# Attention stage of a two-block layer: softmax reciprocals through DRAM, one product per pair of heads

## The chip, the cores and the metric

One core of one Trainium2 chip runs the whole program. The metric is device time in microseconds (us). Names of engines: PE is TensorE's matmul side and PEld its weight loads, DVE is VectorE, ACT is ScalarE, POOL is GpSimd, SP is SyncE, which here issues nearly all DMAs.

## What is computed

The reference is a gated-linear-attention block followed by a second block with two attentions, a convolutional feed-forward layer and norms, on 1024 tokens of width 1024. The change lies in the two attentions of the second block, where each of 8 + 8 heads does, per block of 128 queries,

```python
sc = jnp.where(causal, sc, -jnp.inf)        # or the mask of the 256 selected keys
p = jax.nn.softmax(sc, axis=-1)
o = jnp.einsum('bhqs,bshd->bqhd', p.astype(v.dtype), v)
```

The kernel leaves the division by the softmax sum until after the product with v: with e = exp(sc - max) and l = sum(e), it computes o = (e v) / l.

## The kernel before

The attention stage is `attend` (L1590). It walks over 64 items. An item is a pair of heads (4 pairs of attention "attB", then 4 of "attA"), a head h of the pair and a pair tp of query tiles (t = 2 tp + w, w = 0 or 1), taken in the order tp = 3, 0, 2, 1. Four steps follow each other in a pipeline:

- `stage_a` (two items ahead): the scores of 128 queries in a PSUM tile `pb` of two banks, a DVE pass that adds the mask and takes the row's extreme (L1637 without a loaded mask, L1639 with one, which for attA comes from DRAM by the DMA of L1804 into a ring `mb` of 4), and on ACT the exponential with its row sum (L1640). The row sums go to a column tile `l`.
- `stage_c`, per chunk of 256 keys: up to four 128x128 transposes on PE (L217, the helper `tr`) into a PSUM tile `ps` of a ring of two, and the split of the result into a high and a low part `pt` (ring of 8). In one chunk of three ACT and DVE do this alone (L1658, L1659), in the other two ACT or DVE copies it to a tile of the ring `r2` (L1662) and POOL makes both parts (L1663, L1664).
- `stage_d`, three chunks later: products with v (L1680), collected in `pg` or `po`.
- `finish` (L1686), once per head and half of the queries, 32 times in all: it adds the two halves of `po` (L1693 on ACT, L1695 on DVE), takes the reciprocal of four columns of `l` (L1697), and multiplies. As `l` has queries on partitions and the output `oT` has them along its row, the reciprocals are first spread: four matmuls against the identity with the reciprocal column broadcast as weights (L1700) into a tile of the ring `ps`, a copy to a tile `R` of the ring `r2` (L1702, ACT), and the product on POOL (L1703).

Rings are pools of buffers: an instruction that writes a buffer waits until the last reader of its former content is done. A scheduler fixes each engine's order at build time; on the chip every engine runs its list in order, and so does SP with its DMAs. Behind the stage comes `branches` (L1850), whose first work is the split of the attention outputs (L1865 on ACT, L1867 on DVE and POOL) and which loads gates by DMA (L1875).

Of the kernel before, what the change touches and what calls it, by code (L numbers as in the profile page):

```python
# [6 lines left out]
F32 = mybir.dt.float32  # L7
# [5 lines left out]
OP = mybir.AluOpType  # L13
PSUM = bass.MemoryType.PSUM

P = 128
T = 1024
D = 1024
NT = T // P
# [135 lines left out]
class K:  # L155
# [1434 lines left out]
    def attend(self, jobs, begun, fill):  # L1590

        nc = self.nc

        order = (3, 0, 2, 1)
        items = [(pair, tp, h) for pair in range(4 * len(jobs)) for h in range(2) for tp in order]
        states, live = {}, {}  # L1600
        states[0], todo = begun

        def setup():
            if todo:
                self.ph = "attT"
                todo.pop(0)()
        while todo:
            setup()

        def job(pair):  # L1610
            self.ph = jobs[pair // 4][0]
            return jobs[pair // 4]

        def stage_a(i, w):

            pair, tp, h = items[i]
            if (tp, h, w) == (order[0], 0, 1) and pair + 1 < 4 * len(jobs):
                states[pair + 1], steps = job(pair + 1)[1]((pair + 1) % 4)
                todo.extend(steps)
            t = 2 * tp + w  # L1620
            _, _, score, bias, _, _ = job(pair)
            live["b", pair, t] = bias(t)
            n = self.nk(t)
            off, chunks = self.key_chunks(n)
            z = self.ps2()[:, off:]
            score(states[pair], h, t, z, chunks)
            b = live["b", pair, t]
            if b is None:
                nc.tensor.matmul(z[:, n - P:n], self.idb, self.cb[:, t], start=False, stop=True, skip_group_check=True)
            place, bank = {0: 0, 3: 1, 1: 0, 2: 1}[tp], tp in order[2:]  # L1630
            p, mn = self.g4(), self.col(1, "mn")
            if (place, w) == (1, 1):
                live["l", pair, h, bank] = self.col(4, "l")
            l = live["l", pair, h, bank]
            j = place * 2 + w
            if b is None:
                nc.vector.tensor_scalar(p[:, :n], z[:, :n], 1.0, None, op0=OP.mult, op1=OP.min, accum_out=mn)  # L1637
            else:
                nc.vector.tensor_tensor_reduce(p[:, :n], z[:, :n], b[:, :n], 1.0, 3.0e38, OP.add, OP.min, mn)  # L1639
            nc.scalar.activation(p[:, :n], p[:, :n], AF.Exp, scale=-1.0, bias=mn, accum_out=l[:, j:j + 1])  # L1640
            live["p", i, w] = p

        def tiles(i, c):

            _, tp, _ = items[i]
            return [(s, [w for w in range(2) if s * P < self.nk(2 * tp + w)]) for s in (2 * c, 2 * c + 1)]

        def stage_c(i, c):
            job(items[i][0])
            pt, n = self.ps(), 0  # L1650
            for s, ws in tiles(i, c):
                for w in ws:
                    self.tr(pt[:, n:n + P], live["p", i, w][:, s * P:(s + 1) * P])
                    n += P
            hi, lo = [self.tq.tile([P, 512], F32R, tag="pt", name=self.nm("pt"), bufs=self.bufs["pt"])[:, :n] for _ in range(2)]
            way = (i + c) % 3
            if way == 0:
                nc.scalar.copy(hi, pt[:, :n])  # L1658
                nc.vector.tensor_tensor(lo, pt[:, :n], hi, op=OP.subtract)  # L1659
            else:  # L1660
                x = self.r2()[:, :n]
                (nc.scalar.copy if way == 1 else nc.vector.tensor_copy)(x, pt[:, :n])  # L1662
                nc.gpsimd.tensor_scalar(hi, x, 1.0, 0.0, op0=OP.mult, op1=OP.add)  # L1663
                nc.gpsimd.tensor_tensor(lo, x, hi, op=OP.subtract)  # L1664
            live["pt", i, c] = hi, lo

        def stage_d(i, c):
            pair, tp, h = items[i]
            _, _, _, _, v, _ = job(pair)
            place, bank = {0: 0, 3: 1, 1: 0, 2: 1}[tp], tp in order[2:]  # L1670
            if place == 1 and c == 0:
                live["po"] = self.po() if bank else self.pg()
            po, n = live["po"], 0
            end = self.nk(2 * tp + 1) // P - 1
            x = live.pop(("pt", i, c))
            for s, ws in tiles(i, c):
                o = slice(place * 256 + ws[0] * P, place * 256 + 256)
                w = P * len(ws)
                for j in range(2):
                    nc.tensor.matmul(po[:, o], v(states[pair], h, s), x[j][:, n:n + w], start=(s == 0 and j == 0),  # L1680
                                     stop=(s == end and j == 1), skip_group_check=True)
                n += w
            if s == end and place == 0:
                finish(pair, h, bank)

        def finish(pair, h, bank):  # L1686

            oT, po = job(pair)[5], live.pop("po")
            q = slice(1, 3) if bank else slice(0, 4, 3)
            hs, other = slice(64 * h, 64 * h + 64), slice(64 - 64 * h, 128 - 64 * h)  # L1690
            o = oT[hs, pair % 4].rearrange("p (q t) -> p q t", q=4)[:, q]
            t1, R = self.r2(), self.r2()
            nc.scalar.copy(t1[hs], po[other])  # L1693
            q2 = lambda y: y[hs].rearrange("p (q t) -> p q t", q=2)
            nc.vector.tensor_tensor(o, q2(po), q2(t1), op=OP.add)  # L1695
            rl = self.col(4, "rl")
            nc.vector.reciprocal(rl, live.pop(("l", pair, h, bank)))  # L1697
            pr = self.ps()
            for j in range(4):
                nc.tensor.matmul(pr[hs, j * P:(j + 1) * P], rl[:, j:j + 1].to_broadcast([P, 64]), self.ident,  # L1700
                                 start=True, stop=True)
            nc.scalar.copy(R[hs], pr[hs])  # L1702
            nc.gpsimd.tensor_tensor(o, o, q2(R), op=OP.mult)  # L1703


        for i in range(2):
            for w in (1, 0):
                stage_a(i, w)
            if fill:
                fill.pop(0)()  # L1710
        behind = []
        for i, (pair, tp, h) in enumerate(items):
            nch = self.nk(2 * tp + 1) // 256
            for c in range(nch):
                if i + 2 < len(items):
                    if c == 0:
                        stage_a(i + 2, 1)
                    if c == nch // 2:
                        stage_a(i + 2, 0)
                stage_c(i, c)  # L1720
                behind.append((i, c))
                if len(behind) > 3:
                    stage_d(*behind.pop(0))
            if i % 8:
                setup()
        for x in behind:
            stage_d(*x)
# [291 lines left out]
    def block2_front(self, first):  # L2019

        pool, causal = self.tc.tile_pool, self.causal
        with pool(name=self.nm("kp2"), bufs=1, reuse_waits="tile") as self.kp2:
# [22 lines left out]
                    self.nc.sync.dma_start(self.dbg["mask"], self.maskd)  # L2045
            if self.stop == "topk":
                return
            self.bufs = {"g4": 7, "mb": 4, "pt": 8, "r2": 4}
            with pool(name=self.nm("tq3"), bufs=1, reuse_waits="tile") as self.tq:
                self.attend([job_b, self.block2_a()], (state, steps[6:]),  # L2050
                            self.gate_halves("gA7", lambda: self.g4()[:, :512]))
# [61 lines left out]
```

## Time and profile before

| | us |
|---|---|
| time, median of 3 runs (lowest, highest) | 2461.34 (2451.25, 2475.97) |
| the profiled execution's own time | 2450.84 |
| its span | 2449.0 |
| PE busy over the span | 2310.1 (94%) |
| DVE, ACT, POOL busy | 1421.7, 856.2, 1087.2 |
| the attention stage, first products with v to the last | 1218 to 1523 |

A busy share is a mean over stages with different limits, so the stage of the change is read by itself. An idle time with a releaser says which instruction the engine waited for; only such waits on the engine that sets the pace cost time. PE's weight loads and matmuls overlap, so the time that a group of matmuls holds PE is read from the chain of work, not from the sum of single durations.

### The profile page before, as it was taken

To read this page: it belongs to the slowest core of one execution; us is meant where nothing else is said; L and a number is where in the kernel's file an instruction comes from. 1 tells how busy PE (TensorE), PEld (TensorE's weight loads), DVE (VectorE), ACT (ScalarE), POOL (GpSimd) and SP (SyncE) were. 2 spreads that over 40 slices of the span, in tenths; PEclk is the share of its full clock that TensorE was granted. 3 is DMA by queue.
4 is the path that set the end of the run, shared out by engine and by line. 5 is a ranking of instruction groups with operands and counts; after the bars stand their busy time and mean duration, and the time that the engine had idled before them with its cause. 6 is when DMAs were issued, how large, how long until landed. Compare 5 with 4: busy or idle time off the path is not lost.

```text
span 2449.0 us, 31277 instructions
## 1 busy us (share of the span) xinstructions
PE 2310.1 (94%) x12073; PEld 1909.1 (78%) x12073; DVE 1421.7 (58%) x2151; ACT 856.2 (35%) x1353; POOL 1087.2 (44%) x869
## 2 busy tenths in 40 slices
PE   4999999998898999788999998999999999999997
PEld 3788787786577888666788887788888888888886
DVE  8564457768656467999766666535333333333335
ACT  4454442443313345542366776102211111111111
POOL 5211136554465352335467788530334344443341
PEclk9999999999699999899999999999999999999999
DMA  6222122222332122344420421340111111111112
GB/s 255 90 97 103 73 91 87 82 82 102 129 115 93 68 80 103 143 112 127 155 57 22 119 65 59 110 164 18 69 52 43 49 47 52 52 52 43 52 43 79
DMA packets 119873, 210.44 MB, mean 86 GB/s; under 512 B 45842, under 2 KB 70050, under 8 KB 119330
## 3 DMA queue, kind: packets, MB, share of 16 engines
q1 hardware_dynamic: 119714, 208.34, 24.8%
q8 instruction: 97, 1.59, 0.3%
q14 instruction: 62, 0.51, 0.1%
HBM read 158.46 MB, written 49.84 MB: 85 GB/s over the span
## 4 chain that ended last, share of the span: by engine, by line
PE 54%; DVE 10%; ACT 1%; POOL 1%; issue 1%; DMA 0%; DVEq 0%; POOLq 0%; ACTq 0%; SPq 0%
PE up_pb L1940 5%; PE up_pb L1939 5%; PE up_pb L1938 5%; DVE topk_jk L1550 4%; PE br_ps L1884 3%; PE dn_ps L1993 3%; PE dn_ps L1995 3%; PE dn_ps L1994 3%; DVE topk_r L1547 2%; PE dn_pb L1938 1%; PE dn_pb L1940 1%; PE dn_pb L1939 1%; PE c_ps L242 1%; PE attB_ps L217 1%; PE c_ps L244 1%; PE c_ps L243 1%
## 5 line engine op out<-in xcount | busy, mean ns | idle before, releaser
L1997 DVE TENSOR_TENSOR br_h<-br_h,dn_ps 128x512 f32<-128x512 f32 x176 | 119.6, 685 | 237.5 <-PE dn_ps L1995 237.3
L1976 DVE SCALAR_TENSOR_TENSOR ffn_ws<-up_pb,cols,ffn_ws 128x1023 f32<-128x1023 f32 x66 | 84.5, 1281 | 138.8 <-ACT ffn_ws L1974 138.0
L205 POOL TENSOR_SCALAR up_wh<-up_raw 128x1024 fp32r<-128x1024 f32 x41 | 43.5, 1060 | 272.9 <-PE up_pb L1939 133.9
L210 POOL TENSOR_TENSOR sb_wl<-sb_raw,sb_wh 128x1024 fp32r<-128x1024 f32 x15 | 38.0, 2535 | 189.7 <-ACT sb_wh L209 189.5
L1974 ACT ACTIVATE ffn_ws<-up_pb,cols 128x1024 f32<-128x1024 f32 x33 | 39.9, 1210 | 235.2 <-PE up_pb L1940 235.2
L210 POOL TENSOR_TENSOR up_wl<-up_raw,up_wh 128x1024 fp32r<-128x1024 f32 x41 | 98.5, 2403 | 20.2 <-PE up_pb L1940 17.5
L1938 PE MATMUL up_pb<-br_h,up_wh 128*128 128x512 f32 x264 | 102.7, 389 | 0.0
L1939 PE MATMUL up_pb<-br_h,up_wh 128*128 128x512 f32 x264 | 102.7, 389 | 0.0
L1940 PE MATMUL up_pb<-br_h,up_wl 128*128 128x512 f32 x264 | 102.7, 389 | 0.0
L1938 PE MATMUL up_pb<-op_fh,up_wh 128*128 128x512 f32 x264 | 102.7, 389 | 0.0
L1939 PE MATMUL up_pb<-op_fl,up_wh 128*128 128x512 f32 x264 | 102.7, 389 | 0.0
L1940 PE MATMUL up_pb<-op_fh,up_wl 128*128 128x512 f32 x264 | 102.7, 389 | 0.0
L1548 ACT ACTIVATE topk_r<-topk_r 128x640 bf16<-128x640 bf16 (+1 forms) x64 | 57.4, 898 | 119.6 <-DVE topk_r L1547 119.6
L1981 ACT CAST up_g<-ffn_ws 128x1024 fp32r<-128x1024 f32 x22 | 23.1, 1051 | 176.1 <-PE dn_ps L1994 97.7
L1993 PE MATMUL dn_ps<-dn_wh,up_g 128*128 128x512 f32 x192 | 75.2, 392 | 1.2 <-DVE br_h L1997 1.2
L654 PE MATMUL gla_pb<-QB,gla_X 128*128 128x128 f32 x448 | 68.0, 309 | 8.2 <-DVE QB L641 7.4
L1995 PE MATMUL dn_ps<-dn_wh,up_g 128*128 128x512 f32 x192 | 74.8, 389 | 0.0
L1994 PE MATMUL dn_ps<-dn_wl,up_g 128*128 128x512 f32 x192 | 74.7, 389 | 0.0
L242 PE MATMUL v_ps<-sb_wh,init_hh 128*128 128x256 f32 x256 | 74.3, 291 | 0.0
L244 PE MATMUL v_ps<-sb_wh,init_hl 128*128 128x256 f32 x256 | 74.0, 289 | 0.0
L243 PE MATMUL v_ps<-sb_wl,init_hh 128*128 128x256 f32 x256 | 73.8, 288 | 0.0
L654 PEld LDWEIGHTS gla_pb<-QB,gla_X 128*128 128x128 f32 x448 | 62.6, 218 | 12.5 <-POOL F_ml L762 4.0
(753 smaller groups left out, 7633.5 us busy)
## 6 DMA issues: line engine op xcount, KB each, us to landing
up_raw<-in_wu SPq DMA_DIRECT2D x43, 512.0 KB, 3.4
dn_raw<-in_wu SPq DMA_DIRECT2D x21, 512.0 KB, 3.5
sb_sp<-F_st SPq DMA_DIRECT2D x32, 256.0 KB, 2.0
sb_raw<-in_wu SPq DMA_DIRECT2D x15, 512.0 KB, 4.2
init_X<-in_wada SPq DMA_DIRECT2D x13, 512.0 KB, 5.3
c_raw<-in_wu SPq DMA_DIRECT2D x13, 512.0 KB, 3.5
br_raw<-in_wu SPq DMA_DIRECT2D x12, 512.0 KB, 4.5
bq_raw<-in_wu SPq DMA_DIRECT2D x11, 512.0 KB, 3.8
```

The source lines that it names most:

```text
L210: (nc.gpsimd if pool else nc.vector).tensor_tensor(l, raw, h, op=OP.subtract)
L242: nc.tensor.matmul(po, hh[:, k, ts], wh[:, cs], start=(k == 0), stop=False)
L243: nc.tensor.matmul(po, hh[:, k, ts], wl[:, cs], start=False, stop=False)
L244: nc.tensor.matmul(po, hl[:, k, ts], wh[:, cs], start=False, stop=(k == KT - 1))
L654: self.nc.tensor.matmul(pl[:, cs], X[:, cs], QB[:, cs], start=True, stop=True)
L1938: nc.tensor.matmul(o, wh[:, s], self.hh[h][:, kk], start=(kk == 0), stop=False)
L1939: nc.tensor.matmul(o, wh[:, s], self.hl[h][:, kk], start=False, stop=False)
L1940: nc.tensor.matmul(o, wl[:, s], self.hh[h][:, kk], start=False, stop=(kk == KT - 1))
L1993: nc.tensor.matmul(po, hi[:, ts], wh[:, cs], start=(k == 0), stop=False)
L1994: nc.tensor.matmul(po, hi[:, ts], wl[:, cs], start=False, stop=False)
L1995: nc.tensor.matmul(po, lo[:, ts], wh[:, cs], start=False, stop=(k == 1))
L1997: nc.vector.tensor_tensor(x, x, po, op=OP.add)
```

## The change

`stage_a` now collects the row sums of a whole pair in one tile of 16 columns. With the pair's last exponential, a new function `spread` takes the reciprocal of all 16 columns at once, writes them to DRAM ordered by head and query (4 bytes each, in runs of 32 bytes), and reads them back twice, each head's 1024 values broadcast to 64 partitions, into one tile R of 128x1024. `finish` keeps only the sum of the two halves; with the pair's last half one product of 128x1024 follows, on POOL, for the last pair of all on DVE. R is read with a step of 8 values, since DRAM holds a query's 8 tiles side by side. The rings `mb` and `r2` shrink from 4 to 3 tiles, which makes the room for R.

```diff
-            place, bank = {0: 0, 3: 1, 1: 0, 2: 1}[tp], tp in order[2:]
             p, mn = self.g4(), self.col(1, "mn")
-            if (place, w) == (1, 1):
-                live["l", pair, h, bank] = self.col(4, "l")
-            l = live["l", pair, h, bank]
-            j = place * 2 + w
+            if (tp, h, w) == (order[0], 0, 1):
+                live["l", pair] = self.col(16, "l")
+            l = live["l", pair]
+            j = h * NT + t
...
             live["p", i, w] = p
+            if (tp, h, w) == (order[-1], 1, 0):
+                spread(pair)
+
+        def spread(pair):
+
+            rl = self.col(16, "rl")
+            nc.vector.reciprocal(rl, live.pop(("l", pair)))
+            d = self.dram([2, P, NT], "rld")
+            nc.sync.dma_start(d.rearrange("h q t -> q h t"), rl.rearrange("p (h t) -> p h t", h=2))
+            R = live["R", pair] = self.tq.tile([P, T], F32, tag="R", name=self.nm("R"), bufs=1)
+            for h in range(2):
+                nc.sync.dma_start(R[64 * h:64 * h + 64], bass.AP(tensor=d.tensor, offset=d[h].offset, ap=[[0, 64], [1, T]]))
...
-            t1, R = self.r2(), self.r2()
+            t1 = self.r2()
...
-            rl = self.col(4, "rl")
-            nc.vector.reciprocal(rl, live.pop(("l", pair, h, bank)))
-            pr = self.ps()
-            for j in range(4):
-                nc.tensor.matmul(pr[hs, j * P:(j + 1) * P], rl[:, j:j + 1].to_broadcast([P, 64]), self.ident,
-                                 start=True, stop=True)
-            nc.scalar.copy(R[hs], pr[hs])
-            nc.gpsimd.tensor_tensor(o, o, q2(R), op=OP.mult)
+            if (h, bank) == (1, True):
+                o = oT[:, pair % 4].rearrange("p (t q) -> p t q", t=NT)
+                eng = nc.vector if pair == 4 * len(jobs) - 1 else nc.gpsimd
+                eng.tensor_tensor(o, o, live.pop(("R", pair)).rearrange("p (q t) -> p t q", t=NT), op=OP.mult)
...
-            self.bufs = {"g4": 7, "mb": 4, "pt": 8, "r2": 4}
+            self.bufs = {"g4": 7, "mb": 3, "pt": 8, "r2": 3}
```

On PE, inside the products with v of the first pair of attB (`po` their accumulator, `ps` the transposes' tiles, `pt` the split parts), the kernel before has the four spreading matmuls as row L1700:

```order
L1680 MATMUL attB_po_9518<-attB_pt_9436,attT_vhl_9209 128x256
L1680 MATMUL attB_po_9518<-attB_pt_9462,attT_vhl_9209 128x256
L1700 MATMUL attB_ps_9490<-idr,attB_c_9488 64x128 x4
L1680 MATMUL attB_po_9518<-attB_pt_9463,attT_vhl_9209 128x256
L1680 MATMUL attB_po_9518<-attB_pt_9462,attT_vhl_9209 128x256
```

In the changed kernel the same place (its L1691 is L1680 of before) goes on with the next chunk's transposes:

```order
L1691 MATMUL attB_po_9506<-attB_pt_9434,attT_vhl_9209 128x256
L1691 MATMUL attB_po_9506<-attB_pt_9460,attT_vhl_9209 128x256
L217 MATMUL attB_ps_9497<-idr,attB_g_9395 128x128
L217 MATMUL attB_ps_9497<-idr,attB_g_9386 128x128
L217 MATMUL attB_ps_9497<-idr,attB_g_9395 128x128
L217 MATMUL attB_ps_9497<-idr,attB_g_9386 128x128
L1691 MATMUL attB_po_9506<-attB_pt_9461,attT_vhl_9209 128x256
```

The row of four matmuls is gone, 32 times over the stage, and nothing is added on PE.

On SP, in attA, the changed kernel's queue has the write of the reciprocals (L1649, `rld`) and the two broadcast reads (L1652, `R`) among the loads of masks (L1811, `mb`), where the kernel before has only masks (its L1804):

```order
L1811 DMA attA_mb_12426<-F_maskd_8335 128x640
L1649 DMA attA_rld_12244<-attA_c_12242 128x2x8
L1811 DMA attA_mb_12469<-F_maskd_8335 128x512
L1652 DMA attA_R_12246<-attA_rld_12244 64x1024 x2
L1811 DMA attA_mb_12478<-F_maskd_8335 128x384
L1811 DMA attA_mb_12512<-F_maskd_8335 128x1024
```

Three DMAs per pair are new there, and the reads stand behind a mask load and ahead of others.

On POOL, in the second pair of attB of the changed kernel, the product (L1710) follows the split of v (L1742, L1743) and stands between the two instructions of one chunk (L1674, L1675, which are L1663 and L1664 of before):

```order
L1742 TENSOR_SCALAR attT_vhl_9209<-attT_g_10343 128x16x64
L1743 TENSOR_TENSOR attT_vhl_9209<-attT_g_10343,attT_vhl_9209 128x16x64
L1674 TENSOR_SCALAR attB_pt_10364<-attB_r_10366 128x512
L1710 TENSOR_TENSOR topk_oB_9083<-topk_oB_9083,attB_R_10188 128x1024
L1675 TENSOR_TENSOR attB_pt_10365<-attB_r_10366,attB_pt_10364 128x512
```

Before, the list has four products of 64x512 per pair (L1703) at four places; now it has one of 128x1024. The rows of all engines behind the attention stage are the same in both kernels up to their line numbers, but for the last pair's product, which stands on DVE ahead of the split of the outputs.

## Rows read from the trace of the kernel before

**Rows 1.** The page: span, and each engine's busy time, share and instructions.

```profile
span 2449.0 us, 31277 instructions
PE 2310.1 (94%) x12073; PEld 1909.1 (78%) x12073; DVE 1421.7 (58%) x2151; ACT 856.2 (35%) x1353; POOL 1087.2 (44%) x869
```

**Rows 2.** Windows: length; busy PE, PEld, DVE, ACT, POOL; clock; DMA share, GB/s.

```profile
1218.00:1388.00 170.00, 166.18 (x1225) 147.65 (x1226) 111.85 (x235) 116.91 (x238) 128.02 (x135) 0.98 0.20 56
1388.00:1523.00 135.00, 128.70 (x938) 112.98 (x935) 88.54 (x202) 93.86 (x202) 109.04 (x118) 1.00 0.22 64
1218.00:1523.00 305.00, 294.88 (x2160) 260.63 (x2160) 200.38 (x436) 210.77 (x440) 237.06 (x253) 0.99 0.21 60
```

**Rows 3.** PE's waits, 1218 to 1523: waiter <- releaser: us, times, longest.

```profile
PE attB_pg L1680 <- ACT attB_pt L1658: 1.9, 1, 1.9
PE attB_ps L217 <- ACT attB_r L1702: 1.8, 2, 0.9
...
PE attA_ps L1700 <- ACT attA_r L1662: 1.1, 4, 0.3
...
PE attA_ps L217 <- ACT attA_r L1702: 0.2, 1, 0.2
```

**Rows 4.** The chain of work, 1206 to 1526: start, us, what; first and last full spread.

```profile
1231.16 1.02 PE attB_ps L1700 x8
...
1510.09 1.02 PE attA_ps L1700 x8
```

**Rows 5.** Groups of instructions, 1218 to 1523: count | busy us, mean ns | idle before.

```profile
L1703 POOL TENSOR_TENSOR topk_oB<-topk_oB,attB_r 64x512 f32<-64x512 f32 x16 | 20.5, 1281 | 10.2 <-ACT attB_r L1702 6.8 <-DVE topk_oB L1695 3.0
L1703 POOL TENSOR_TENSOR attT_oA<-attT_oA,attA_r 64x512 f32<-64x512 f32 x15 | 19.3, 1286 | 6.2 <-ACT attA_r L1702 2.8 <-DVE attT_oA L1695 2.6 <-DVE attA_c L1697 0.2
L1702 ACT COPY attB_r<-attB_ps 64x512 f32<-64x512 f32 x16 | 9.3, 580 | 2.7 <-PE attB_ps L1700 1.7 <-POOL attB_pt L1664 0.3
L1736 POOL TENSOR_TENSOR attT_vhl<-attT_g,attT_vhl 128x1024 fp32r<-128x1024 f32 x3 | 7.1, 2375 | 0.2
```

**Rows 6.** POOL's slowest 128x1024 product of the span, and DVE's reciprocals by line.

```profile
L563 POOL TENSOR_TENSOR gs_tmp<-go_qkb,go_qkb 128x1024 f32<-128x1024 f32 x2 | 7.0, 3495 | 3.6 <-DVE go_qkb L798 3.6
L1697 DVE RECIPROCAL attB_c<-attB_c x16: 158/172/179, 1216.8 to 1373.0; 128x4 f32<-128x4 f32 x16
```

**Rows 7.** Waits of ACT's copies: longest for POOL, longest for PE; columns as in 3.

```profile
ACT attA_r L1662 <- POOL attA_pt L1664: 3.2, 2, 2.4
ACT attB_r L1662 <- PE attB_ps L217: 14.5, 12, 3.3
```

**Rows 8.** Timeline of DMA issues and, at the stage's end, of DVE and ACT.

```profile
1539.01 0.27 SPq L299 DMA_DIRECT2D ffn_fd<-fm  x1
1540.14 0.21 SPq L301 DMA_DIRECT2D fr<-ffn_fd  x1
1512.91 0.18 DVE L1697 RECIPROCAL attA_c<-attA_c 128x4 f32<-128x4 f32 x1 [0.78 <-ACT attA_g L1640]
1523.75 0.69 DVE L1695 TENSOR_TENSOR attT_oA<-attA_po,attA_r 64x512 f32<-64x512 f32 x1 [3.21 <-ACT attA_r L1693]
1525.06 6.48 DVE L1867 TENSOR_TENSOR br_ol<-topk_oB,br_oh 128x512 fp32r<-128x512 f32 x4 [0.61 <-ACT br_oh L1865]
1523.75 0.58 ACT L1702 COPY attA_r<-attA_ps 64x512 f32<-64x512 f32 x1
```

**Rows 9.** DMA issue to landing: the masks (min, median, max) and 512 KB loads (median).

```profile
DMA to landing us min/median/max: 1.8/2.4/4.6
attT_F<-x_aqd SPq DMA_DIRECT2D x8, 512.0 KB, 5.0
```

**Rows 10.** DVE's timeline around the mask ring: the release of a slot, its next use.

```profile
1415.56 0.96 DVE L1639 CUSTOM_DVE_ANT_0 attA_g<-attA_pb,attA_mb 128x768 f32<-128x768 f32 x1 [0.22 <-PE attA_pb L1847]
1422.35 0.56 DVE L1639 CUSTOM_DVE_ANT_0 attA_g<-attA_pb,attA_mb 128x384 f32<-128x384 f32 x1 [0.61 <-PE attA_ps L217]
```

**Rows 11.** DVE's 128x1024 product with two operands in SBUF, feed-forward stage.

```profile
L1982 DVE TENSOR_TENSOR up_g<-ffn_ws,up_g 128x1024 fp32r<-128x1024 f32 x22 | 30.1, 1369 | 44.2 <-ACT up_g L1981 44.2
```

## The prediction

> **What bounds the kernel now.** I read the page first, for the whole: PE is busy for 2310 of 2449 us [rows 1], so the program as a whole leans on PE. [...] PE's idle time is 305.0 - 294.9 = 10.1 us, 3%. The third view, PE's waits, names it: 13 rows, none over 1.9 us [rows 3]. The copies that feed POOL wait longest for PE's transposes, 14.5 us [rows 7]. The fourth view, the chain of work, runs through PE for most of the stage, and the spreading matmuls stand in it themselves, 1.02 us a group (8 rows of the trace for 4 matmuls in the code) [rows 4]. So in this stage work taken from PE is time, as long as nobody else takes PE's place.
>
> **The change part by part.**
>
> *Matmuls removed.* 32 groups (8 pairs x 2 heads x 2 halves) hold PE for 1.02 us each [rows 4]: 32.6 us. Nothing comes in on PE.
>
> *Waits removed with them.* The groups also take one of two `ps` tiles and give it back only after ACT's copy. PE waited 1.8 + 0.2 us for that copy and 1.1 us ahead of the groups for their tile [rows 3]: 3.1 us, all gone.
>
> *ACT.* The 32 copies of 0.58 us [rows 5] go: 18.6 us in all, 18.0 of them inside the windows' 305. ACT was not the pace; what is left is 192.8 us.
>
> *POOL.* 31 products of 1.28 us inside the window, 39.8 us [rows 5], give way to 7 of 128x1024. No row shows POOL reading with a step of 8 values. The bound below is the plain 128x1024 row, 2.38 us [rows 5], the one above the slowest 128x1024 row of the span, 3.5 us [rows 6]. I take 2.4, since the size is that row's and only one of two operands has the step. POOL then has 237.1 - 39.8 + 16.7 = 214 us (222 at the upper bound). [...] Neither value moves the sum while PE sets the pace.
>
> *DVE.* 32 reciprocals of 0.17 us [rows 6] become 8 of 16 columns, each between 0.17 and four times that; DVE ends between 196 and 200 us before its one product. Free either way: DVE has over 70 us of slack. The reciprocal waits for the pair's last exponential, as its predecessor did, but 8 times and not 32.
>
> *The round trip.* It is not on PE's path if R lands before POOL reaches the product. Below: a write of a few bytes and a read that hangs on it were issued 1.13 us apart [rows 8], and the shortest mask load landed after 1.8 us [rows 9], so 3.2 us with the issue. Above: 4.6 us, the slowest mask load, for the write, 5.0 us, the median of a 512 KB load, for the two reads of 256 KB [rows 9], and about 1.5 us of issue and of standing behind a mask load: 11. I take 7. The cover: in the last pair the reciprocal was taken at 1512.9 and the last sum ended at 1524.4 [rows 8], 11.5 us later, and in the other pairs PE has further items between the two. It is hidden; without that cover POOL would stand for it, and `pt`, three chunks deep, would hide some 3 x 305 / 160 = 5.7 us of that (160 chunks in the stage) before PE stands too.
>
> *SP's queue.* Three DMAs more per pair. Behind the reads stand mask loads for DVE. The ring of masks is shorter by one: a slot released at 1416.5 is used next, three masks on, at 1422.35 [rows 10], 5.8 us for a load of 2.4, at worst 4.6 [rows 9]. The read waits for the write's landing, about 1 us longer than the mask load ahead of it waits for its slot. 5.8 less 2.4 leaves 3.4 for it. Cost zero; up to 2 us in each of the 4 attA pairs if the slowest landing meets the wait, 8 us.
>
> *The ring r2.* It loses a tile and 32 of its 138 + 32 writers (106 copies, 32 `t1`, 32 `R`). Copies waited little for POOL so far, 3.2 us in the longest row [rows 7]. Per tile and writer there were 4 x 305 / 170 = 7.2 us, and there will be 3 x 277 / 138 = 6.0. Some of this comes back as waits of ACT and DVE and, behind them, of PE. With the other engines' shares after the change (POOL 214 of 277, 77%; ACT 70%; DVE 71%) hardly above today's (78, 69, 66%), I let PE's remaining waits double: 10.1 - 3.1 = 7.0 us more. Bounds: none, and the case of the second rival.
>
> *The stage's end.* ACT starts the split of the outputs 0.58 us earlier, as its last copy is gone. DVE, which started its own split at 1525.06, 0.6 us after its last sum [rows 8], now has the product in between: 1.4 us by the plain row [rows 11], 3.2 at the pace of its own split beside POOL's, 6.48 us for 4 of 512 [rows 8]. That is 0.8 to 2.6 us later, on an engine for which PE waits soon after. I take +1.0, bounds -0.6 and +2.6.
>
> *Sum.* -32.6 - 3.1 + 7.0 + 1.0 = -27.7 us against the profiled execution's 2450.84: 2423.1. Without any waits coming back and with the better end it is 2414.5. The profiled execution stands 10.5 us under the median of the runs. I don't know which of the two the changed kernel's runs will resemble and put half of that on top, 5.2: 2428.
>
> **The rivals.**
>
> *POOL keeps its waits.* If POOL with the shorter ring becomes what the others wait for, its idle time, 305.0 - 237.1 = 67.9 us, doesn't shrink, and the stage lasts 214 + 67.9 = 282 us, with the upper price 222 + 67.9 = 290: 15 to 23 us gained, or 2429 to 2437 against the profiled execution with the end's 1.0, and 2434 to 2442 on the scale of the forecast. For it: in attA POOL is at 81% already [rows 2], and a product behind a split of v holds POOL for some 6 us at one stroke. Against it: copies have waited for POOL for little [rows 7], and the copies that POOL waits for stand waiting for PE [rows 7]. [...]
>
> *PE was not the pace.* PE's busy time is modelled. Were the matmuls only filling time in which scores wait for exponentials, the stage would stay at 305 us: 2451, or 2456 on the forecast's scale. Against it: only 10.1 us of idle PE [rows 2], and copies that wait for PE [rows 7].
>
> *R comes late (the other side).* POOL's list is in order. If R lands after POOL's product is due, all chunks behind it wait, then PE. It costs beyond the 5.7 us of `pt`, and to eat 4.1 us (32.6 / 8) per pair the wait must be 9.8 us: a round trip of 11.5 + 9.8 = 21 us decides. At 25 us the kernel is 8 x 4 = 32 us slower than that point, 2488. For it: the read stands behind mask loads on SP. Against it: 11 us was the upper bound.
>
> **How the numbers follow.** The forecast has 0.62 with a range of its own of 2414 to 2434; POOL's rival 0.26; PE not the pace 0.07; R late 0.05. A change of 1%, about 24.6 us, is what a measurement of this kernel can tell from none. The forecast gains more than that, the two next gain less, the last loses: faster 0.62, same 0.33, slower 0.05. The range from 2413, all gained and no offset, to 2446, POOL's rival with its slow end and a few us of late masks, leaves out about 2 in 10.
>
> **What would show it.** In the changed kernel's windows the stage should last about 277 us with PE busy for 262 and idle for about 14. The 7 POOL products should read 2.4 us; at 3.5 the step costs. POOL's waits for R should be absent, and DVE's for masks too. PE's waits should name L1673's copies and L1669 more often than before. I am wrong if PE's idle time passes 20 us (the ring or POOL), if POOL shows a wait for a DMA of R (the round trip), or if the stage's end is later relative to PE's last product by over 3 us.

## The result, and the profile after

The changed kernel takes 2436.38 us (median of 4 runs, 2427.9 to 2442.5) beside 2463.47 us of the kernel before on the same chip (4 runs, one more than in the table ahead): the ratio is 0.9897, 95% interval 0.9855 to 0.9939. A second comparison, of 5 runs with 21 of the kernel before, gave 2432.71 us beside 2459.62, ratio 0.989, interval 0.9871 to 0.9909. So the change gains 27 us, 1.1%, and with the narrower interval 22 to 32 us.

| | before, us | after, us |
|---|---|---|
| profiled execution, its span | 2450.84, 2449.0 | 2427.90, 2426.0 |
| start of the attention stage (first product with v) | 1218.3 | 1230.7 |
| the stage's length | 304.8 | 270.5 |
| PE busy, idle in it | 295.0, 9.8 | 259.9, 10.6 |
| from its last product with v to the span's end | 925.9 | 924.8 |

The page of the changed kernel, where PE, ACT and POOL have less work and DVE as much as before [rows 1]:

```profile
span 2426.0 us, 30675 instructions
PE 2279.7 (94%) x11817; PEld 1881.1 (78%) x11817; DVE 1423.4 (59%) x2128; ACT 837.9 (35%) x1321; POOL 1066.1 (44%) x844
```

The windows over the changed kernel's stage: attB, attA, both (length; busy PE, PEld, DVE, ACT, POOL; clock; DMA share, GB/s), beside [rows 2]:

```profile
1230.70:1378.90 148.20, 144.49 (x1079) 129.22 (x1080) 107.99 (x219) 103.70 (x216) 115.70 (x121) 1.00 0.30 75
1378.90:1501.18 122.28, 115.43 (x828) 101.71 (x826) 89.23 (x195) 88.96 (x193) 102.93 (x109) 1.00 0.33 93
1230.70:1501.18 270.48, 259.92 (x1904) 230.93 (x1904) 197.22 (x413) 192.67 (x408) 218.63 (x229) 1.00 0.32 83
```

PE has 256 matmul rows less, 35 us less busy time, and as little idle time as before: the stage became shorter by what was taken from PE. PE's longest remaining waits in the changed kernel, beside [rows 3] (its L1669, L1670, L1673, L1636 and L1638 are L1658, L1659, L1662, L1637 and L1639 of before; L1796 and L1853 are score matmuls):

```profile
PE attB_pg L1691 <- ACT attB_pt L1669: 1.9, 1, 1.9
PE attA_po L1691 <- POOL attA_pt L1675: 1.8, 3, 0.8
PE attA_ps L217 <- DVE attA_pt L1670: 1.7, 4, 1.0
PE attA_pb L1853 <- DVE attA_c L1638: 1.1, 3, 0.4
PE attB_pb L1796 <- DVE attB_g L1636: 1.0, 3, 0.3
```

The waits for the spread's copy are gone, and no wait of PE names R or a mask. Summed over all rows of the two stages, PE's waits for POOL's parts went from 0.6 to 2.8 us, for DVE's parts from 0.7 to 2.0 and for DVE's passes over the scores from 0.3 to 2.1; those for the copies into `r2` (L1662 before, L1673 after) fell from 3.7 to 1.4. DVE waited for masks twice, 1.6 us in all; the kernel before has no such wait.

**Where 34 us in the stage and 23 us between the two profiled executions part.** The stage of the changed kernel starts 12.4 us later, though all that runs before it is the same code. The windows from the span's start to the stage's start, of the kernel before:

```profile
0.00:1218.30 1218.30, 1108.30 (x5913) 900.66 (x5914) 850.82 (x1300) 490.47 (x743) 499.44 (x397) 0.96 0.32 110
```

and of the changed kernel:

```profile
0.00:1230.70 1230.70, 1114.34 (x5914) 904.04 (x5914) 852.55 (x1299) 490.40 (x743) 497.78 (x397) 0.95 0.32 109
```

The counts are the same but for one or two, the clock is a hundredth lower and PE's busy time 6 us longer. Over all 14 profiled executions of this study the same stretch ended between 1218.3 and 1246.7 us, and the kernel before had the earliest of them. The six executions of the kernel before and of kernels built on it have a mean of 1229.2 us there, the eight of the changed kernel and of those built on it 1229.6: nothing shows that the change moves the start, and it is the profiled execution of the kernel before that was early. Spans of single executions are therefore no measure of a change of 1%; below, lengths of the stage and ratios over many runs are compared.

### The profile page after: what moved, and what is told of

Same layout as the page of the kernel before. It is cut to its first block, busy times and chain, and to the rows that moved or that the text cites. A ratio compares the mean times of both kernels' runs of the same rounds, so it can differ in the third digit from the quotient of the medians.

```text
span 2426.0 us, 30675 instructions
## 1 busy us (share of the span) xinstructions
PE 2279.7 (94%) x11817; PEld 1881.1 (78%) x11817; DVE 1423.4 (59%) x2128; ACT 837.9 (35%) x1321; POOL 1066.1 (44%) x844
## 4 chain that ended last, share of the span: by engine, by line
PE 47%; DVE 10%; issue 2%; POOL 1%; ACT 1%; DMA 0%; SPq 0%; DVEq 0%; POOLq 0%; ACTq 0%
PE up_pb L1946 5%; PE up_pb L1945 5%; PE up_pb L1947 5%; DVE topk_jk L1550 4%; PE br_ps L1891 3%; PE dn_ps L2000 3%; PE dn_ps L2001 3%; PE dn_ps L2002 3%; DVE topk_r L1547 2%; PE dn_pb L1947 1%; PE dn_pb L1946 1%; PE dn_pb L1945 1%; PE op_ps L1085 1%; PE op_ps L1086 1%; PE op_ps L1087 1%
## 5 line engine op out<-in xcount | busy, mean ns | idle before, releaser
L1988 ACT CAST up_g<-ffn_ws 128x1024 fp32r<-128x1024 f32 x22 | 23.1, 1049 | 176.0 <-PE dn_ps L2001 97.7
```

## The experiments

Stage lengths (first to last product with v) with PE's busy and idle time, each from one profiled execution, and the ratio to the kernel before over the runs. The clock is the mean of what TensorE was granted, as a share of full speed. The two executions of the changed kernel show how far one profile can be trusted: their stages differ by 3.9 us, all of it busy time at another clock, and their idle times by 0.1.

| kernel | stage | PE busy | PE idle | clock | ratio [95%] |
|---|---|---|---|---|---|
| before | 304.8 | 295.0 | 9.8 | 0.99 | |
| after | 270.5 | 259.9 | 10.6 | 1.00 | 0.9897 [0.9855, 0.9939] |
| after_again | 274.4 | 263.9 | 10.5 | 0.98 | 0.9890 [0.9871, 0.9909] |
| spread_twice | 328.2 | 319.4 | 8.8 | 1.00 | 1.0126 [1.0095, 1.0157] |
| spread_bf16 | 295.7 | 278.8 | 16.9 | 0.98 | 0.9972 [0.9953, 0.9992] |
| both_reliefs | 291.3 | 275.3 | 16.0 | 0.99 | 0.9968 [0.9945, 0.9990] |
| mm_back | 281.6 | 273.5 | 8.1 | 0.99 | 0.9928 [0.9878, 0.9978] |
| ring_back | 287.2 | 275.5 | 11.7 | 1.00 | 0.9938 [0.9913, 0.9963] |
| copy_back | 272.5 | 261.7 | 10.8 | 1.00 | 0.9897 [0.9855, 0.9939] |
| rings_only | 303.1 | 292.5 | 10.6 | 1.00 | 1.0029 [1.0009, 1.0049] |
| pool_relief | 303.9 | 294.7 | 9.2 | 0.99 | 1.0021 [0.9995, 1.0047] |
| dve_products | 277.0 | 258.9 | 18.1 | 0.99 | 0.9908 [0.9878, 0.9937] |
| two_hops | 273.8 | 264.3 | 9.5 | 0.98 | 0.9913 [0.9882, 0.9945] |
| rows_q | 313.9 | 272.5 | 41.4 | 0.94 | 1.0046 [1.0021, 1.0072] |

### Is PE the pace, and does the gain repeat?

The changed kernel once more, without an edit, and the kernel before with each spreading matmul issued twice:

```diff
-                for j in range(4):
+                for j in (0, 1, 2, 3, 0, 1, 2, 3):
```

> The changed kernel as it is, timed again. Theory (PE is the pace of the attention stage, and the stage gives back all of the matmuls' time): from the first product with v to the last 271 us against 305 before, with PE idle for about 11; the time 30 to 36 us under the kernel before, ratio 0.986, since the 12.4 us by which the profiled execution of the change was late before the stage began belong to that execution alone. Rival (the change itself makes the start of the program slower by some 12 us): the stage begins near 1230 us again and the ratio stays at 0.990.

> The kernel before, with each of the four spreading matmuls of a group issued twice: 256 more on the trace's count, everything else as it was. Theory (PE is the pace): the stage grows by all of the 32 x 1.02 = 32.6 us, ratio 1.013, PE's idle time stays near 10 us. Rival (PE had slack, its busy time is filling): the stage grows by less than half of that and PE's idle time shrinks.

The gain repeated, but not as expected: the ratio is 0.989 and not 0.986, and the stage begins at 1230.6 us again, the two signs that I had named for the rival. The means above speak against that rival all the same: the start near 1230 us is the usual one. The expectation had taken the changed kernel's execution for a late one, where the kernel before's was early. The stage of the second profile is 30.4 us shorter than before; why the medians gain 27 stays open.

Doubling the spread cost 1.26%, 23.4 us in the stage against the profiled kernel before, of the 32.6 expected. The stage of spread_twice, and that of rings_only (below), in the columns of [rows 2]:

```profile
1222.90:1551.08 328.18, 319.36 (x2416) 286.65 (x2416) 200.22 (x436) 210.68 (x439) 237.57 (x253) 1.00 0.20 56
...
1233.90:1536.98 303.08, 292.45 (x2162) 258.41 (x2161) 200.19 (x436) 210.49 (x439) 236.63 (x253) 1.00 0.21 60
```

The chain of work of spread_twice shows a doubled group at 1.89 us (16 rows), where [rows 4] had 1.02 for 8:

```profile
1233.58 1.89 PE attB_ps L1700 x16
1244.31 1.89 PE attB_ps L1700 x16
```

The second four cost 0.87 us, 32 times 27.8; the stage took 23.4 of it against the kernel before and 25.1 against rings_only, which does the same PE work at a full clock. PE's idle time fell by 1 us. Work added to PE in this stage is time, nearly one for one: the rival "PE was not the pace" is out.

### Is it the matmuls' time alone?

The kernel before with spreads in bf16 keeps every step and changes only what the matmuls cost; both_reliefs does this and moves the products from POOL to DVE as well (`nc.vector.tensor_tensor(o, o, q2(R), op=OP.mult)`):

```diff
-            rl = self.col(4, "rl")
+            rl = self.cp.tile([P, 4], BF16, tag="rlb", name=self.nm("c"), bufs=3)
...
-                nc.tensor.matmul(pr[hs, j * P:(j + 1) * P], rl[:, j:j + 1].to_broadcast([P, 64]), self.ident,
+                nc.tensor.matmul(pr[hs, j * P:(j + 1) * P], rl[:, j:j + 1].to_broadcast([P, 64]), self.idb,
```

> The kernel before, with reciprocals, identity and spreading matmuls in bf16; the same copies, products, rings and waits, so that only PE's time for the 32 groups shrinks. The division's precision is lower, no part is left out. Theory (PE's time alone is the gain): a group falls from 1.02 us to about 0.3, so the stage gains 32 x 0.7 = 23 us, ratio 0.991. Rival (the gain came from POOL's and ACT's load and from the ring of transposes, which this kernel leaves as they were): under 10 us.

> bf16 spreading matmuls and the 32 products on DVE together. Theory (PE's relief alone gave 7 us because POOL, whose load it left, paced attA; the change gains since it takes from both): PE's idle time falls back from 17 towards 10 us and the stage gains 18 to 23 us against the kernel before, ratio 0.991 to 0.993. Rival (the bf16 kernel fell short because of the scheduler's other order and the two clock dips that its profile shows, not because of POOL): the ratio stays at 0.997.

PE's busy time fell by 16.2 us (by the chain of work a group went from 1.02 to 0.34 us, 21.8 in all, but the granted clock was 0.98 against 0.99), the stage by only 9.1, and the time by 0.3%. The expected 23 us and 0.991 did not come; the number is the rival's, under 10 us. The other 7.1 us came back as idle time of PE. Its waits in spread_bf16 (L1703 is the copy, L1702 of before):

```profile
PE attA_pg L1680 <- POOL attA_pt L1664: 4.4, 8, 1.0
PE attB_ps L217 <- ACT attB_r L1703: 2.6, 2, 2.0
PE attA_po L1680 <- POOL attA_pt L1664: 2.0, 4, 1.0
```

Here PE's idle time does rise, as I had forecast for the change itself. The rows suggest POOL. But with POOL relieved of 33 us (both_reliefs, POOL busy 203.4 us in the stage) PE is still idle for 16.0 us, and the longest waits name DVE:

```profile
PE attA_pb L1847 <- DVE attA_c L1639: 2.6, 4, 0.8
PE attA_ps L217 <- DVE attA_pt L1659: 2.2, 3, 1.3
PE attA_po L1680 <- POOL attA_pt L1664: 2.0, 4, 0.8
```

The stage is 13.5 us shorter than before, not the expected 18 to 23, and the ratio stays at 0.997, the rival's. It is no clean test of POOL's load, though: the products give DVE 24.5 us more (225.0 against 200.5), and DVE's are the waits that came in.

So a shorter spread is worth about a quarter of what its removal is worth. Three kernels look for the rest from the other end: the changed kernel with one piece put back into `finish` each time, its result unused. Four small bf16 matmuls into a `ps` tile, the same with ACT's copy behind them, and a copy alone:

```diff
+            pr = self.ps()
+            for j in range(4):
+                nc.tensor.matmul(pr[other, j * P:(j + 1) * P], self.idb[:, j:j + 1].to_broadcast([P, 64]), self.idb,
+                                 start=True, stop=True)
```

mm_back is these lines; ring_back has this one behind them:

```diff
+            nc.scalar.copy(t1[other], pr[other])
```

and copy_back this one alone:

```diff
+            nc.scalar.copy(t1[other], t1[hs])
```

> The changed kernel with four small bf16 matmuls (identity by identity, result unused) put back in each of the 32 finishes, into a `ps` tile that nobody copies. The earlier run with bf16 spreads showed such a group at about 0.38 us on PE. Either theory (PE paces; the ring and the copy carry the rest): PE busy and stage +8 to +14 us over the changed kernel's 270.5 to 274.4, so 280 to 287 us; against the kernel before about 0.994 to 0.996. If the tile of `ps` taken out of turn is itself dear even without a copy: stage 290 us or more, ratio 0.998 and above.

> The same with ACT's 64x512 copy out of the `ps` tile behind the matmuls (result unused, into the free half of t1), so that the tile comes free only after ACT. Theory `ring and copy`: what bf16 spreads left of the change's gain, some 20 us, is half matmul time and half waits for this copy; the stage is 292 to 298 us (as with bf16 spreads, 295.7) with PE idle about 17, ratio 0.997 to 1.000. Rival `other`: the rest came from the order or from the products, not from the copy; the stage is 280 to 287 us as without the copy, PE idle 10 to 12, ratio 0.994 to 0.996.

> The changed kernel with only ACT's load put back: one more 64x512 copy (0.58 us, 18.6 us in all) per finish, from SBUF to SBUF, with no matmul and no `ps` tile. If ACT's time itself carried the part beside the matmuls: stage +8 to +12 us, 280 to 285, ratio 0.993 to 0.995. If it is the `ps` tile held during the copy, or neither: stage within 3 us of the changed kernel's 270.5 to 274.4, ratio 0.989 to 0.991.

A bf16 group holds PE for 0.34 us, as the chain of work of ring_back shows:

```profile
1417.78 0.34 PE attA_ps L1709 x4
1428.58 0.34 PE attA_ps L1709 x4
```

32 of them are 10.9 us, and mm_back's stage is 11.1 us longer than the changed kernel's (7.2 longer than in its second profile). With the copy that then holds the `ps` tile, ring_back's stage is 5.6 us longer still: 2.0 busy and 3.6 idle. Its PE waits name the new copy, L1711, for 2.6 us:

```profile
PE attA_ps L217 <- ACT attA_r L1711: 1.4, 4, 0.5
...
PE attB_ps L217 <- ACT attB_r L1711: 1.2, 2, 1.0
```

Copy_back, with the same 18.6 us more on ACT (211.7 us busy) but no `ps` tile behind it, has a stage of 272.5 us, 2.0 longer, and the changed kernel's ratio. ACT's time costs nothing that these runs can tell. That a `ps` tile held while ACT copies costs something is suggested by the named 2.6 us, and not shown: PE's idle time in ring_back, 11.7 us, is only 1.1 over the changed kernel's. The expectation "292 to 298 us" for ring_back fell: it came out at the upper edge of its rival. By ratio, mm_back and ring_back can't be told apart (0.9928 and 0.9938 with overlapping intervals); the 5.6 us rest on one profile each, and two profiles of one kernel differ by 3.9.

Read in a row, the stages make a ladder: 270.5 (after), 281.6 (bf16 groups back), 287.2 (with the copy), 295.7 (spread_bf16), 304.8 (before). The steps are 11.1 for the presence of groups, 5.6 for the ring's copy, 8.5 between ring_back and spread_bf16, and 9.1 for groups in f32 rather than bf16. Of the 8.5, PE's busy time is 3.3, for the same matmuls at a clock of 0.98 in place of 1.00; 5.2 is idle time. What causes that part stays open: the two kernels differ in the products per half on POOL, in 32 reciprocals tied to them, in the rings, and in the order that the scheduler gives. both_reliefs speaks against POOL's load alone, as far as a kernel can that loads DVE instead.

### Do the shorter rings or the place of the products matter?

The kernel before with the rings `mb` and `r2` cut to 3 tiles, the kernel before with its 32 products on DVE, and the changed kernel with all its products on DVE:

```diff
-            self.bufs = {"g4": 7, "mb": 4, "pt": 8, "r2": 4}
+            self.bufs = {"g4": 7, "mb": 3, "pt": 8, "r2": 3}
...
-            nc.gpsimd.tensor_tensor(o, o, q2(R), op=OP.mult)
+            nc.vector.tensor_tensor(o, o, q2(R), op=OP.mult)
...
-                eng = nc.vector if pair == 4 * len(jobs) - 1 else nc.gpsimd
+                eng = nc.vector
```

> The kernel before with the rings of masks and of r2 cut from 4 to 3 tiles, alone. Theory: r2 still has 170 writers here, and a tile is asked for again after 3 x 305 / 170 = 5.4 us; ACT's and DVE's copies wait for POOL for some us more, PE hardly: 0 to 8 us slower, ratio 1.000 to 1.003. Rival (rings set the pace of the split): 15 us or more slower, with PE's waits naming copies.

> The kernel before with its 32 products of 64x512 on DVE in place of POOL; spreading matmuls, copies and rings as before. Theory (PE paces the stage before, and POOL becomes the next pace within some 10 us of it): POOL loses 41 us of work and nothing is gained, 0 to 5 us, ratio 0.998 to 1.000, as PE's work stays at 295 us in the stage. Rival (POOL's load was a pace of its own beside PE): 10 us or more.

> The changed kernel with all 8 products on DVE (2.1 us each, as the last pair's) and none on POOL (3.05 us each). Theory (after the change POOL waits for PE and PE for POOL about evenly, PE's idle time is 11 us of 271): POOL loses 21 us of work and 1 to 4 us are gained, ratio to the kernel before 0.987 to 0.989. Rival (DVE, whose passes over the scores feed the exponentials, is late by each product): 3 us or more slower than the change.

rings_only has a stage of 303.1 us, no longer than before, with PE idle for 10.6 us against 9.8, though its runs are 0.3% slower; where those 7 us lie, its one profile doesn't show. pool_relief gains nothing: POOL has 36 us less in the stage, and the stage is 303.9. That speaks against the rival in which POOL's waits set the length. dve_products is not better either: the expected 1 to 4 us did not come, the stage is 277.0 us, PE idles for 18.1 us, and the largest waits name POOL:

```profile
PE attA_pg L1691 <- POOL attA_pt L1675: 4.3, 5, 1.4
PE attA_pg L1691 <- POOL attA_pt L1674: 2.1, 3, 1.1
```

POOL in turn waited 15.4 us for DVE's copies (L1673), against 7.0 in the changed kernel, and was idle for 66.2 us against 51.9: the products on DVE held up the copies that POOL's chunks need. No placement beat the changed kernel's; by ratio, dve_products and the change can't be told apart.

### How much room has the round trip?

two_hops lets the reciprocals take one more step through DRAM; rows_q writes them in the order of the tokens, in pieces of 4 bytes, so that the product reads R without a step:

```diff
+            d2 = self.dram([2, P, NT], "rld2")
+            nc.sync.dma_start(d2, d)
+            d = d2
...
-            d = self.dram([2, P, NT], "rld")
-            nc.sync.dma_start(d.rearrange("h q t -> q h t"), rl.rearrange("p (h t) -> p h t", h=2))
+            d = self.dram([2, NT, P], "rld")
+            nc.sync.dma_start(d.rearrange("h t q -> q (h t)"), rl)
...
-                eng.tensor_tensor(o, o, live.pop(("R", pair)).rearrange("p (q t) -> p t q", t=NT), op=OP.mult)
+                eng.tensor_tensor(o, o, live.pop(("R", pair)).rearrange("p (t q) -> p t q", t=NT), op=OP.mult)
```

> The changed kernel with a second hop in DRAM (a DRAM-to-DRAM copy between the write of the reciprocals and the reads of R), so that R lands some 3 to 5 us later and SP's queue waits once more per pair. If the round trip has the slack that the changed kernel's trace shows (R issued 13 us ahead of its product): POOL shows no wait for R, the stage stays within 3 us of 270.5 to 274.4, ratio 0.988 to 0.992. If the slack is nearly used up or the masks behind it on SP are: DVE waits for masks of 2 us and more, the stage is 5 to 15 us longer, ratio 0.992 to 0.996.

> The changed kernel with the reciprocals written to DRAM with the query innermost, as single 4-byte pieces, so that the product reads R without a step. Theory: the POOL product falls from 3.05 us to the 2.4 of rows without a step (the step's price is 0.65 us, 27%), DVE's last product from 2.1 to 1.4; the write lands later, by some us, which the 8 us between its landing and the product hide; 0 to 4 us gained against the change, ratio to the kernel before 0.987 to 0.989. Rival (the write of 2048 pieces lands so late that POOL waits for R): POOL shows waits for the DMA of R and the kernel is slower than the change.

First the changed kernel itself, in the first pair. DVE's timeline (start, length), SP's and POOL's:

```profile
1254.42 0.25 DVE L1647 RECIPROCAL attB_c<-attB_c 128x16 f32<-128x16 f32 x1 [0.78 <-ACT attB_g L1639]
...
1254.70 0.36 SPq L1649 DMA_DIRECT2D attB_rld<-attB_c  x1
...
1258.10 1.16 SPq L1652 DMA_DIRECT2D attB_R<-attB_rld  x2
...
1271.15 3.13 POOL L1710 TENSOR_TENSOR topk_oB<-topk_oB,attB_R 128x1024 f32<-128x1024 f32 x1
```

From issue to landing, the changed kernel's writes (its L1649; 6 of the 8 have a landing in the trace):

```profile
DMA to landing us min/median/max: 1.5/3.2/3.7
```

and its reads (L1652; 7 of 16), with the first and last issue of those in attB and in attA:

```profile
L1652 SPq DMA_DIRECT2D attB_R<-attB_rld x8: 450/552/597, 1258.1 to 1374.4; - x8
L1652 SPq DMA_DIRECT2D attA_R<-attA_rld x8: 450/520/590, 1402.4 to 1494.2; - x8
...
DMA to landing us min/median/max: 3.4/3.9/4.8
```

In the first pair the second read is issued at 1258.7 us and lands after 4.8, at 1263.5: 9.1 us after the reciprocal and 7.7 ahead of the product. Other pairs have less room. The last read of attB is issued at 1374.4, 7.5 us ahead of its product (1381.9), which leaves 2.7 us at the slowest landing and 4.1 at the fastest; the last of attA, issued at 1494.2, landed after 4.1 us, 4.2 ahead of DVE's product at 1502.5. two_hops fits in there: its second hop lands after 1.9 us, POOL waits for no R, and the stage stays at 273.8 us. Little of the room is left then: in the last pair of attB the read issued at 1379.1 lands after 4.0 us, 2.2 ahead of the product at 1385.3.

rows_q loses 43 us in the stage against the changed kernel. Its write lands after (2 of the 8 are in the trace):

```profile
DMA to landing us min/median/max: 9.4/10.2/11.0
```

The reads stand on SP until then, and all loads behind them. Waits of SP's queue, of POOL and of DVE in rows_q:

```profile
SPq L1652 <- DMA attB_rld<-attB_c: 41.9, 4, 11.4
...
SPq L1652 <- DMA attA_rld<-attA_c: 26.3, 3, 9.6
...
POOL attT_vhl L1742 <- DMA attT_g<-x_vBd: 23.1, 3, 8.5
...
DVE attA_g L1638 <- DMA attA_mb<-F_maskd: 14.2, 4, 5.7
```

and what its products (L1710) waited for:

```profile
  DMA attA_R<-attA_rld: 8.2, 2
```

R itself is late twice, for 8.2 us together: 2.4 on POOL in the stage, and 5.7 on DVE behind its last product with v. v is late for 23.1 us and masks for 14.2. PE's two longest waits are for the split of v and for DVE's pass over masked scores:

```profile
PE attB_pg L1691 <- POOL attT_vhl L1743: 10.5, 2, 6.7
PE attA_pb L1853 <- DVE attA_c L1638: 9.9, 8, 4.1
```

PE then idles for 41.4 us, and its busy time grows by 12.6 for the same matmuls at a clock of 0.94. In the changed kernel SP stood for 11.8 us behind the writes (7.3 and 4.5 for the two attentions), here for 68.2.

## Why the prediction was right, and where it wasn't

**Direction and mechanism: right.** PE paces the stage; the groups' 32.6 us came off it. PE's busy time fell by 35.0 us, by 31.1 in the second profile of the changed kernel, at a clock of 0.98, and by 32.5 against rings_only, which has the groups and the clock of the first profile, 1.00.

**Size: right, in part by luck.** The time lies in the stated range, 8 us above the point. It lies above the forecast's own 2414 to 2434, though, and inside the 2434 to 2442 that I gave POOL's rival: the time alone can't choose between them. The stage can: the rival had it at 282 to 290 us with POOL idle for 67.9; it lasted 270.5 and 274.4, with POOL idle for 51.9 and 55.7. That the sum's 27.7 us and the medians' 27 agree so closely is luck. The sum gives the stage 28.7 of them, where the two profiles show 34.3 and 30.4, and no run settles where the difference to the medians lies (their narrower interval, 22 to 32 us, holds the second value and not the first).

**"PE's remaining waits double, 7.0 us more": too much.** PE's idle time went from 9.8 to 10.6 us. With 3.1 us removed, 3.9 came back, not 7.0. The path was another too: I had them come by the ring `r2` and its copies, and looked for L1673 and L1669 in PE's waits. Those rows fell, from 3.7 to 1.4 us and from 2.7 to 1.9; what came in names POOL's parts, DVE's parts and DVE's passes over the scores. I had multiplied today's waits without asking what the change takes from the engines that PE waits for. spread_bf16, which shortens PE's work and leaves all else, has an idle PE (16.9 us); why it has and the change hasn't is not shown in full: ring_back, with matmuls and copy put back, idles for 11.7.

**The stage's end: too small to read.** I put +1.0; the rest of the program after the last product with v is 1.1 us shorter in the first profile of the changed kernel, and as long as before, 925.9 us, in the second. Over the 14 executions it takes 923.6 to 928.0 us, whatever the change, so no sign can be read from it. Timeline of the changed kernel's end, beside [rows 8]:

```profile
1502.47 0.50 PE L1891 MATMUL br_ps<-br_oh,br_wh 128*128 128x512 f32 x1 [1.31 <-ACT br_oh L1872]
1502.54 2.11 DVE L1710 TENSOR_TENSOR attT_oA<-attT_oA,attA_R 128x1024 f32<-128x1024 f32 x1
...
1504.56 1.79 DVE L1874 TENSOR_TENSOR br_ol<-topk_oB,br_oh 128x512 fp32r<-128x512 f32 x1
```

The product takes 2.11 us, between my bounds of 1.4 and 3.2, and DVE's split begins 3.4 us after the last product with v (2.0 before). But PE waits first for the first high part from ACT, which now comes 0.6 us sooner, and later for DVE's low parts 1.5 us in two waits. The term was priced on DVE alone, where PE's next wait was for ACT.

**POOL's product: between the bounds, on neither.** In the changed kernel:

```profile
L1710 POOL TENSOR_TENSOR topk_oB<-topk_oB,attB_R x4: 2858/3039/3133, 1271.2 to 1381.9; 128x1024 f32<-128x1024 f32 x4
L1710 POOL TENSOR_TENSOR attT_oA<-attT_oA,attA_R x3: 2993/3082/3092, 1413.9 to 1475.9; 128x1024 f32<-128x1024 f32 x3
```

and in rows_q, the same product without the step:

```profile
L1710 POOL TENSOR_TENSOR topk_oB<-topk_oB,attB_R x4: 2359/2368/2382, 1278.3 to 1410.6; 128x1024 f32<-128x1024 f32 x4
L1710 DVE TENSOR_TENSOR attT_oA<-attT_oA,attA_R x1: 1225/1225/1225, 1550.9 to 1550.9; 128x1024 f32<-128x1024 f32 x1
```

The step of 8 values, in one of two operands, cost 28% on POOL: 3.03 us a product on average over the seven, 2.37 without it. POOL came to 218.6 us, 5 over the estimate; what these 5 us cost no run shows alone, and all of PE's waits for POOL came to 2.8 us.

**Round trip: right for this change, but the rival behind it had the wrong mechanism.** I put 7 us with 11.5 of cover. Measured were 6.3 to 9.1 us in the four pairs whose landing is in the trace, with 10.7 of cover in the last pair, and R was never waited for. My rival priced a late R by POOL's list and set its point of decision at 21 us. In rows_q the reads land about 17 us after the reciprocal, short of that point, and the whole gain is lost all the same. The cost ran over SP's queue, which I had at zero to 8 us: the reads at its head waited for the writes, up to 11.4 us at a time, and of the loads behind them v was late for 23.1 us and masks for 14.2, where R was late for 8.2.

**From the profile to the median: the step that put the point off.** I added half of the 10.5 us by which the kernel before's profiled execution stood under its median. That execution reached the stage earliest of all 14, at 1218.3 us where the mean is 1229, so it was no usual one, and the whole offset belonged on top: 2461.3 less the 27.7 would have been 2433.6, nearer to 2436.4 than 2428. The changed kernel's own two profiled executions stand 8.5 us under their median and on it. (The range's lower end, 2413, is also 1.5 us under the 2414.5 of the sum that it goes by.)

**Settled and open.** Settled: PE is the pace; R is in time in every pair, with some 3 us of room at the least; ACT's load alone costs the changed kernel nothing that can be told; and POOL's products, moved to DVE, gain nothing in the kernel before or the changed one. By one profile, the shorter rings cost the stage of the kernel before nothing. Open: what the `ps` tile held by a copy costs, 5 us of PE's idle time between ring_back and spread_bf16, where the medians' gain falls short of the first profile's stage, why rings_only's runs are 0.3% slower, and what sets the scatter of the code ahead of the stage.

## What to carry to other kernels

In a stage where one engine is busy for 97% of the time, see first whether its instructions can be taken away rather than made cheaper: by the runs, removal brought 27 us here where a cheaper form of the same matmuls brought 7, as 7.1 us of what PE saved came back as waits, for reasons that are settled only in part. A small round trip through DRAM was cheap here while its landing (3.2 us for the write, 3.9 for the reads, medians) was short against the distance to its use (10.7 us from reciprocal to product in the last pair), but price it by the queue that it stands in, not only by its own consumer: in rows_q SP stood behind the writes for 68.2 us, and the gain was gone. Compare changes of 1% by the stage's own length and by medians of many runs; the span of one profiled execution also carries what the clock did elsewhere.

## What the runs showed of the hardware that I had not expected

A write of 8 KB from SBUF to DRAM landed after 3.2 us (median) in runs of 32 bytes and after 10.2 us in pieces of 4 bytes. On DVE the 128x1024 product took 2.11 us when one operand had a step of 8 values (2.08 to 2.85 for the eight of dve_products) and 1.23 us, once, without. The same instructions ahead of the stage took from 1218.3 to 1246.7 us in 14 executions, with the granted clock of 340 to 580 us at 0.97 in the kernel before and at 0.93 in the changed one:

```profile
340.00:580.00 240.00, 224.19 (x1319) 186.26 (x1316) 179.54 (x172) 86.40 (x99) 134.53 (x70) 0.97 0.24 85
```

```profile
340.00:580.00 240.00, 226.68 (x1288) 187.80 (x1288) 171.27 (x165) 85.20 (x97) 126.11 (x67) 0.93 0.23 81
```

In the same 240 us the first has 31 matmul rows more. What lowered the clock there no run shows.
